# One encoder layer in fp32: attention steps grouped anew, VectorE's order written out at the start of the first FFN, its last four pairs narrow

## The chip, the cores and the metric

The kernel runs on one core of a Trainium2 chip. The metric is the device time of one execution in microseconds (us), the median of several runs. TensorE (PE) does the matmuls into eight PSUM banks, ScalarE (ACT) and VectorE (DVE) work on what lies in SBUF and PSUM, GpSimd (POOL) and SyncE (SP) mostly issue DMAs.

## The reference

One layer on 512 tokens of width 1024: a SwiGLU FFN of hidden width 2816 at half weight, two attention branches side by side, and a second FFN. Each sub-layer has an RMSNorm before and after.

```python
def _swiglu(x, w_gate, w_up, w_down):
    return (jax.nn.silu(x @ w_gate) * (x @ w_up)) @ w_down
...
        f = _swiglu(_rmsnorm(x, ffn1_pre_g[l]), ffn1_w_gate[l], ffn1_w_up[l], ffn1_w_down[l])
        x = x + 0.5 * _rmsnorm(f, ffn1_post_g[l])
        h = _rmsnorm(x, mix_pre_g[l])
        proj = h @ w_in[l]
        qa, ka, va, qb, kb, vb, gate_a, gate_b = jnp.split(proj, splits, axis=-1)
        ha = (B, T, NA_HEADS, HEAD_DIM)
        ya = _neighbourhood_attention(qa.reshape(ha), ka.reshape(ha), va.reshape(ha), na_rpb[l]) @ w_branch_a[l]
        yb = _dilated_mixture(qb, kb, vb, slopes) @ w_branch_b[l]
        merged = jax.nn.sigmoid(gate_a) * ya + jax.nn.sigmoid(gate_b) * yb
        x = x + _rmsnorm(merged @ w_out[l], mix_post_g[l])
        f = _swiglu(_rmsnorm(x, ffn2_pre_g[l]), ffn2_w_gate[l], ffn2_w_up[l], ffn2_w_down[l])
        x = x + 0.5 * _rmsnorm(f, ffn2_post_g[l])
```

The neighbourhood branch has 8 heads of width 64, the dilated one 12 heads in three groups with dilations 1 (the near group), 4 and 16 (the far groups). All values are float32.

## The kernel before, in words

**Arithmetic.** Every fp32 operand is split into a rounded part `hi` and a rest `lo`: ACT casts `hi` (L116) and DVE subtracts it (L117). A product is then three matmuls, hi x hi, hi x lo and lo x hi (`mm3`, L207 to L209).

**FFN, gate and up.** Of the 22 blocks of hidden features (each 128 wide) the first two are computed in the plain way (`proj_first`, `proj_into`). The other 20 go through `seven`: each gate and up projection is treated as a 2 x 2 block product done with seven block products instead of eight, numbered 1 to 7. Their left sides are sums of weight blocks, made partly by DMAs that add onto what they load (POOL, L407 and L408) and partly by DVE in `sums_of` (L413 `t2`, L415 or L418 `t4`). `ready(j, i)` splits block i of pair j; `product(j, i, ...)` runs it. A pair keeps two banks, `q` and `p`. Product 5 starts `p`, ACT copies it (L496) and product 3 adds onto it. Products 6 and 7 and then 4 add onto `q`; DVE reads `q` after product 7 (L490) before product 4 goes on. In the first FFN pairs 0 to 3 have their product 1 done ahead (`first_products`), into four banks.

A *wide* product (5 and 3 alone) has the hi and lo halves of its moving side next to each other: four matmuls of 512 columns (L458) and four of 256 (L460), and DVE then has two more adds a pair (L492, L514). A *narrow* one is twelve matmuls of 256 columns. In the first FFN pairs 0 to 3 are narrow and 4 to 19 wide (`state["narrow"] = 4`), in the second all are wide.

**FFN, down.** `down` does the down projection in the same seven-product way, in class `Blocks`. While the last pairs run, `behind(lead)` and `behind(far)` load and split its first blocks. The rows `ta`, `tb`, `ba`, `bb` are kept in the room of the normalised input `hn`, whose last reader is product 4 of the last pair. For block product 6 DVE adds the rows `ba` onto `ta` (L749); the sums of tokens `v` are L739.

**Attention.** Work of the attention is put in a list, `pend`, as small steps; `step(n)` takes n of them. Between two projections (24 matmuls of 512 columns each) `pair` calls `step`. A step is a burst of scores for two heads (`na_sc`, `g_sc`: 24 matmuls on 64 rows, L1099, four banks, which DVE drains in eight L1106), the transposes of one head's probabilities (`na_tr`, L1133, two banks) or its product with the values (`na_pv`, L1160, one bank). Scores of the far groups (`scores_narrow`, L1071) take two banks a head. An empty step is written as a function that does nothing. `v_far` projects the values of the far groups into four banks, `v_near` those of the near group.

**Order.** A planner lays out each engine's instructions by a simulated timeline, with program order as priority. Stretches in the list `ordered` keep the written order on PE, ACT and DVE; entries of `pool` keep it for the engines that they name; SP keeps it up to the end of the first FFN. `mark()` notes a place in the program.

Of the kernel before, what the change touches and what calls it, by code (L numbers as in the profile page):

```python
# [24 lines left out]
NF = 2816 // P  # L25
# [4 lines left out]
WIDE = (5, 3)  # L30
# [5 lines left out]
STD = 2  # L36
# [10 lines left out]
def block_kernel(ctx, tc, x, gains, weights, rpb_near, rpb_all, alibi0, alibi12, out):  # L47
# [13 lines left out]
    def unit(dt=F32, name="u"):  # L61
        return up.tile([P, 512], dt, tag="u", name=name)
# [61 lines left out]
    ordered = []  # L124
    pool = []
# [65 lines left out]
    def mark():  # L191
        return len(nc.cur_bb.bb.instructions)
# [229 lines left out]
        split(w[:, :512], w[:, 512:], raw)  # L422
        return w

    def seven(use, mv, n_pairs, n0, behind, far, lead, raws, early):

        blocks = {}
        o = {}

        def get(j):
            if j < n_pairs and j > 2:
                raws[j] = load_blocks(n0, j)
            elif j >= n_pairs:
                behind(far)

        def ready(j, i):  # L440
            if j < n_pairs:
                if j and loads:
                    loads.popleft()()
                if i == 1:
                    sums_of(raws[j])
                if j >= EARLY or i not in (1, 2):
                    blocks[j, i] = split_block(raws[j].pop(i))
            else:
                behind(lead)

        def product(j, i, key, start):
            if start:
                o[key, j] = bank(key)
            w = blocks.pop((j, i))
            acc = o[key, j][:, :256]
            if i in WIDE and j >= state["narrow"]:
                for k in range(4):
                    nc.tensor.matmul(o[key, j], w[:, k * P:(k + 1) * P], mv[i][k][2], start=start and k == 0, stop=False,  # L458
                                     skip_group_check=True)
                    nc.tensor.matmul(acc, w[:, 512 + k * P:512 + (k + 1) * P], mv[i][k][0], start=False,  # L460
                                     stop=k == 3, skip_group_check=True)
                return o[key, j]
            for k in range(4):
                mm3(acc, w[:, k * P:(k + 1) * P], w[:, 512 + k * P:512 + (k + 1) * P], *mv[i][k][:2],
                    start and k == 0, k == 3, skip_group_check=True)
            return acc

        res = {}
        get(0)
        get(1)  # L470
        for i in (1, 5, 2, 6, 3, 7, 4):
            ready(0, i)
        for j in range(n_pairs + 1):
            now, was = j < n_pairs, j > 0
            get(j + 2)
            if now:
                if j < EARLY:
                    o["q", j], g = early[j]
                    q = o["q", j][:, :256]
                else:  # L480
                    q = product(j, 1, "q", True)
                    g = unit(name="g")
                    nc.scalar.copy(g[:, :256], q)
                u = unit(name="up")
                res[j] = g, u, u[:, 256:] if j < state["narrow"] else unit(name="p5")
            ready(j + 1, 1)
            if was:
                q0 = product(j - 1, 7, "q", False)
                g0, u0, s0 = res.pop(j - 1)
                nc.vector.tensor_tensor(u0[:, 256:], s0[:, :256], q0, op=ALU.subtract)  # L490
                if j > state["narrow"]:
                    nc.vector.tensor_tensor(u0[:, 256:], u0[:, 256:], s0[:, 256:], op=ALU.add)  # L492
            ready(j + 1, 5)
            if now:
                p = product(j, 5, "p", True)
                nc.scalar.copy(res[j][2], p)  # L496
            ready(j + 1, 2)
            if now and j >= EARLY:
                r = product(j, 2, "r", True)
                nc.vector.tensor_tensor(g[:, :256], g[:, :256], r, op=ALU.add)  # L500
            ready(j + 1, 6)
            if now:
                product(j, 6, "q", False)
                nc.scalar.copy(u[:, :256], q)
            ready(j + 1, 3)
            if was:
                product(j - 1, 4, "q", False)
                use(j - 1, g0, u0, q0)
            ready(j + 1, 7)
            if now:  # L510
                product(j, 3, "p", False)
                nc.vector.tensor_tensor(u[:, :256], p[:, :256], u[:, :256], op=ALU.subtract)  # L512
                if j >= state["narrow"]:
                    nc.vector.tensor_tensor(u[:, :256], p[:, 256:], u[:, :256], op=ALU.add)  # L514
            ready(j + 1, 4)

# [74 lines left out]
    def ffn(g, store, src):  # L591
# [20 lines left out]
        def use(j, pg, pu):  # L612
            h = unit(name="h")
            nc.scalar.activation(h, pg, AF.Silu)
            times(j, pu, h)

        def use7(j, g, u, q):
            if j >= EARLY:
# [14 lines left out]
        for j in range(STD):  # L633
            ps = [bank(), bank()]
            for i in range(2):
                (proj_into if i or j else proj_first)(ps[i], take(False), 0, T)
                next(sums)
                if j < STD - 1:
                    fetch()
            use(j, *ps)  # L640
            if j == 0:
                ordered[-1].append(mark())
        g_post, g_pre = gain(g), None if store else gain(g + 1)
        if not store:
            bias_plan()
# [2 lines left out]

        far, lead, rest = down(m, after, duos, hidden, g_post, g_pre, store, src)
        state["next"] = state["take"] = after + 2 * m + 2  # L650
        state["narrow"] = 0 if store else 4
        seven(use7, mv, NF - STD, n0, lambda q: [f() for f in q.popleft()], far, lead, raws, early)
        rest()

    def parts_of(raw):
# [564 lines left out]
    def mixing(g):  # L1220
# [48 lines left out]
        def na_use(p, pq, pk):  # L1269
            if p < 3:  # L1270
                load_tables(na_tab[p + 1], 3, bias_f[:, (p + 1) * 1536:(p + 2) * 1536])
            parts = qk_parts("na", pq, pk)
            for h in (2 * p, 2 * p + 1):
                pend.append((lambda: None) if h % 2 else lambda h=h: na_sc(parts, h))
                if h > 0:
                    pend.append(lambda h=h: na_tr(h - 1))
                if h > 1:
                    pend.append(lambda h=h: na_pv(h - 2))


        g_tab = {0: [], 1: [], 2: [], 3: []}
# [34 lines left out]
        def g_use(j, pq, pk):  # L1316
            g, p = divmod(j, 2)
            parts = qk_parts(g, pq, pk)
            for h in (2 * p, 2 * p + 1):
                pend.append((lambda: None) if g == 0 and h % 2 else lambda h=h: g_sc(g, parts, h))  # L1320

        def g_tr(g, h):
            pr = hold.pop(("p", g, h))
# [9 lines left out]
        vva += next(v_na)  # L1333
        g_post, g_pre = gain(g), gain(g + 1)
        pair(na_use, 2, 1)
        pair(na_use, 3, 3)
        pend.append(lambda: na_tr(7))
        pend.append(lambda: na_pv(6))
        pend.append(lambda: na_pv(7))
        load_tables(g_tab[0], 3, alibi0[:, :1536])  # L1340
        load_tables(g_tab[1], 3, alibi0[:, 1536:])
        load_tables(g_tab[2], 1, alibi12[:, :512])
        load_tables(g_tab[3], 1, alibi12[:, 512:])
        for j in range(6):
            pair(g_use, j, 1 if j else 3)
        pend.append(lambda: joint(1))
        vvb[1], vvb[2] = v_far()
        vvb[0] = v_near()
# [413 lines left out]
```

## Time and profile before

| | |
|---|---|
| Median of 3 runs | 1078.69 us (1078.28 to 1079.77) |
| Profiled execution, whole | 1078.63 us |
| Its span, first to last instruction | 1076.9 us |
| Mean granted TensorE clock | 0.999 |
| PE busy | 1067.4 us (99%), 6403 matmuls |
| DVE busy | 845.1 us (78%) |
| ACT busy | 650.9 us (60%) |

A row of the timeline gives the start and the duration in us, the engine, the line, the operation and what it writes and reads; in brackets stands the idle time of the engine before it and what ended that. Matmuls overlap, so the time that one costs is read from the start of the next and not from its duration. The pairs of the first FFN lie at 46 to 245 us, its down projection from 233 on, the attention's projections at about 345 to 560, the second FFN from about 742.

### The profile page before, as it was taken

What the parts mean: (1) busy time and instruction counts of PE and PEld (TensorE: products, weight loads), DVE (VectorE), ACT (ScalarE), POOL (GpSimd) and SP (SyncE); (2) the same over time, 40 slices, a digit from 0 to 9 for tenths busy, and PEclk for the clock granted to TensorE, in tenths of its full rate; (3) what the DMA queues carried; (4) which work ended last, traced back from release to release, by engine and by line L of the source; (5) the groups of instructions that cost most, each with busy time, mean ns of one, the idle gap of its engine ahead of it and who ended that gap; (6) DMA issues with size and microseconds to landing.
All of it is one profiled execution on the core that took longest, in us unless ns stands there. A gap on an engine that the chain in (4) does not pass through costs nothing.

```text
span 1076.9 us, 17914 instructions
## 1 busy us (share of the span) xinstructions
PE 1067.4 (99%) x6403; PEld 949.6 (88%) x6403; DVE 845.1 (78%) x1632; ACT 650.9 (60%) x1312; POOL 179.4 (17%) x247
## 2 busy tenths in 40 slices
PE   9999999999999999999999999999999999999997
PEld 7899999997888988888988888889899999998886
DVE  7989888878997667666677654777998888889985
ACT  7646665664784656556676651366655665666672
POOL 4111212014334000000000001133302111104301
PEclk9999999999999999999999999999999999999999
DMA  9979888569994453422232239575938777769962
GB/s 330 198 185 248 218 225 219 148 163 278 231 276 125 125 184 127 135 82 79 80 95 89 79 100 306 139 139 191 292 76 206 190 171 195 192 190 237 221 211 78
DMA packets 95724, 189.80 MB, mean 176 GB/s; under 512 B 24081, under 2 KB 26641, under 8 KB 95634
## 3 DMA queue, kind: packets, MB, share of 16 engines
q1 hardware_dynamic: 68320, 134.18, 36.9%
q0 software_dynamic: 24624, 54.01, 28.1%
q8 instruction: 50, 0.82, 0.3%
q10 hardware_dynamic: 2690, 0.46, 0.2%
q14 instruction: 40, 0.33, 0.1%
HBM read 183.58 MB, written 7.58 MB: 178 GB/s over the span
## 4 chain that ended last, share of the span: by engine, by line
PE 92%; DMA 3%; DVE 2%; SPq 2%; issue 1%; ACT 1%; DVEq 0%; ACTq 0%
PE q L209 11%; PE q L207 11%; PE q L208 11%; PE ps L207 10%; PE ps L208 10%; PE ps L209 10%; PE p L458 6%; PE p L460 3%; PE r L209 3%; PE r L208 3%; PE r L207 3%; PE c L209 2%; PE c L207 2%; PE c L208 2%; SPq L1190 1%; PE ps L1133 1%
## 5 line engine op out<-in xcount | busy, mean ns | idle before, releaser
L117 DVE TENSOR_TENSOR w<-raw,w 128x512 fp32r<-128x512 f32 (+1 forms) x138 | 125.6, 915 | 91.9 <-ACT w L116 88.8
L116 ACT CAST w<-raw 128x512 fp32r<-128x512 f32 (+1 forms) x138 | 110.0, 803 | 93.6 <-PE ps L208 44.1
L207 PE MATMUL ps<-hn,w 128*128 128x512 f32 (+1 forms) x360 | 136.5, 379 | 0.3
L209 PE MATMUL ps<-hn,w 128*128 128x512 f32 (+1 forms) x360 | 134.6, 374 | 0.0
L208 PE MATMUL ps<-hn,w 128*128 128x512 f32 (+1 forms) x360 | 134.3, 373 | 0.0
L116 ACT CAST w<-t 128x512 fp32r<-128x512 f32 x160 | 97.5, 619 | 44.3 <-DVE t L413 28.6
L117 DVE TENSOR_TENSOR w<-t,w 128x512 fp32r<-128x512 f32 x160 | 109.3, 690 | 13.5 <-ACT w L116 11.2
L458 PE MATMUL p<-v,w 128*128 128x512 f32 x288 | 104.5, 397 | 0.0
L208 PE MATMUL q<-v,w 128*128 128x256 f32 x320 | 90.4, 283 | 0.0
L207 PE MATMUL q<-v,w 128*128 128x256 f32 x320 | 90.4, 283 | 0.0
L209 PE MATMUL q<-v,w 128*128 128x256 f32 x320 | 90.0, 283 | 0.0
L407 POOL DMA_DIRECT2D t<-in_weights_dram x40 | 35.0, 874 | 285.5 <-DVE up L512 58.9
L208 PE MATMUL q<-hn,w 128*128 128x256 f32 x288 | 81.6, 283 | 0.0
L209 PE MATMUL q<-hn,w 128*128 128x256 f32 x288 | 81.6, 283 | 0.0
L207 PE MATMUL q<-hn,w 128*128 128x256 f32 x288 | 81.3, 283 | 0.0
L460 PE MATMUL p<-v,w 128*128 128x256 f32 x288 | 80.7, 281 | 0.0
L209 PEld LDWEIGHTS ps<-hn,w 128*128 128x128 f32 x360 | 67.8, 188 | 12.7 <-DVE w L117 0.7
L207 PEld LDWEIGHTS ps<-hn,w 128*128 128x128 f32 x360 | 67.9, 189 | 11.9 <-DVE nast L1106 0.7
L208 PEld LDWEIGHTS ps<-hn,w 128*128 128x128 f32 x360 | 67.9, 189 | 11.0
L458 PEld LDWEIGHTS p<-v,w 128*128 128x128 f32 x288 | 54.2, 188 | 9.6
L207 PEld LDWEIGHTS q<-v,w 128*128 128x128 f32 x320 | 60.9, 191 | 0.3
L208 PEld LDWEIGHTS q<-v,w 128*128 128x128 f32 x320 | 61.0, 191 | 0.1
(328 smaller groups left out, 3015.7 us busy)
## 6 DMA issues: line engine op xcount, KB each, us to landing
raw<-in_weights_dram SPq DMA_DIRECT2D x90, 512.0 KB
t<-in_weights_dram SPq DMA_DIRECT2D x88, 256.0 KB
t<-in_weights_dram POOLq DMA_DIRECT2D x80, 256.0 KB, 5.7
w<-in_weights_dram SPq DMA_DIRECT2D x40, 256.0 KB
rows<-in_weights_dram SPq DMA_DIRECT2D x32, 256.0 KB
w<-in_weights_dram POOLq DMA_DIRECT2D x32, 256.0 KB, 6.3
tb<-in_weights_dram POOLq DMA_DIRECT2D x12, 512.0 KB, 7.7
rows<-in_weights_dram POOLq DMA_DIRECT2D x24, 256.0 KB, 10.9
```

Source lines behind the costliest of these rows:

```text
L116: nc.scalar.copy(hi, src)
L117: nc.vector.tensor_tensor(lo, src, hi.bitcast(F32), op=ALU.subtract)
L207: nc.tensor.matmul(o, sh, mh, start=start, stop=False, **kw)
L208: nc.tensor.matmul(o, sh, ml, start=False, stop=False, **kw)
L209: nc.tensor.matmul(o, sl, mh, start=False, stop=stop, **kw)
L407: nc.gpsimd.dma_start(t1, weights[gate][:, :512], accum_op=ALU.add)
L458: nc.tensor.matmul(o[key, j], w[:, k * P:(k + 1) * P], mv[i][k][2], start=start and k == 0, stop=False, skip_group_check=True)
L460: nc.tensor.matmul(acc, w[:, 512 + k * P:512 + (k + 1) * P], mv[i][k][0], start=False, stop=k == 3, skip_group_check=True)
L1133: nc.tensor.transpose(ps[:, i * P:(i + 1) * P], s, ident)
L1190: nc.sync.dma_start(bias_r[i][:, r, :].rearrange("h (u k) -> h u k", k=8), (rpb_near, rpb_all)[i][:, :, 7 - r:15 - r])
```

## The change

- In `seven` the first pair's block 5 is split ahead of the pair's sums, and `put`, the last multiplication of the plain blocks (`times`, L603), goes between the splits of blocks 3 and 7. Before, it stood ahead of all of them. This holds for both FFNs.
- In the first FFN alone DVE keeps the written order from the first plain block to the second pair's sums (`pin`).
- `state["wide"]` takes the place of `state["narrow"]`: in the first FFN pairs 4 to 15 are wide, 16 to 19 are narrow now; the second stays wide throughout.
- The neighbourhood branch's steps are grouped by a written plan, one group between two projections, and the empty steps of the near group go. By that plan bursts of scores stand in groups of their own.

```diff
--- before.py
+++ after.py
@@ -422,7 +422,7 @@
         split(w[:, :512], w[:, 512:], raw)
         return w
 
-    def seven(use, mv, n_pairs, n0, behind, far, lead, raws, early):
+    def seven(use, mv, n_pairs, n0, behind, far, lead, raws, early, put, pin):
 
 
 
@@ -453,7 +453,7 @@
                 o[key, j] = bank(key)
             w = blocks.pop((j, i))
             acc = o[key, j][:, :256]
-            if i in WIDE and j >= state["narrow"]:
+            if i in WIDE and j in state["wide"]:
                 for k in range(4):
                     nc.tensor.matmul(o[key, j], w[:, k * P:(k + 1) * P], mv[i][k][2], start=start and k == 0, stop=False,
                                      skip_group_check=True)
@@ -468,8 +468,13 @@
         res = {}
         get(0)
         get(1)
-        for i in (1, 5, 2, 6, 3, 7, 4):
+        blocks[0, 5] = split_block(raws[0][5])
+        ready(0, 1)
+        raws[0].pop(5)
+        for i in (6, 3, 7, 4):
             ready(0, i)
+            if i == 3:
+                put()
         for j in range(n_pairs + 1):
             now, was = j < n_pairs, j > 0
             get(j + 2)
@@ -482,13 +487,15 @@
                     g = unit(name="g")
                     nc.scalar.copy(g[:, :256], q)
                 u = unit(name="up")
-                res[j] = g, u, u[:, 256:] if j < state["narrow"] else unit(name="p5")
+                res[j] = g, u, unit(name="p5") if j in state["wide"] else u[:, 256:]
             ready(j + 1, 1)
+            if pin and j == 0:
+                pool.append((pin, mark(), (mybir.EngineType.DVE,)))
             if was:
                 q0 = product(j - 1, 7, "q", False)
                 g0, u0, s0 = res.pop(j - 1)
                 nc.vector.tensor_tensor(u0[:, 256:], s0[:, :256], q0, op=ALU.subtract)
-                if j > state["narrow"]:
+                if j - 1 in state["wide"]:
                     nc.vector.tensor_tensor(u0[:, 256:], u0[:, 256:], s0[:, 256:], op=ALU.add)
             ready(j + 1, 5)
             if now:
@@ -510,7 +517,7 @@
             if now:
                 product(j, 3, "p", False)
                 nc.vector.tensor_tensor(u[:, :256], p[:, :256], u[:, :256], op=ALU.subtract)
-                if j >= state["narrow"]:
+                if j in state["wide"]:
                     nc.vector.tensor_tensor(u[:, :256], p[:, 256:], u[:, :256], op=ALU.add)
             ready(j + 1, 4)
 
@@ -612,7 +619,7 @@
         def use(j, pg, pu):
             h = unit(name="h")
             nc.scalar.activation(h, pg, AF.Silu)
-            times(j, pu, h)
+            return lambda: times(j, pu, h)
 
         def use7(j, g, u, q):
             if j >= EARLY:
@@ -637,9 +644,12 @@
                 next(sums)
                 if j < STD - 1:
                     fetch()
-            use(j, *ps)
+            put = use(j, *ps)
+            if j < STD - 1:
+                put()
             if j == 0:
                 ordered[-1].append(mark())
+        pin = None if store else ordered[-1][1]
         g_post, g_pre = gain(g), None if store else gain(g + 1)
         if not store:
             bias_plan()
@@ -648,8 +658,8 @@
 
         far, lead, rest = down(m, after, duos, hidden, g_post, g_pre, store, src)
         state["next"] = state["take"] = after + 2 * m + 2
-        state["narrow"] = 0 if store else 4
-        seven(use7, mv, NF - STD, n0, lambda q: [f() for f in q.popleft()], far, lead, raws, early)
+        state["wide"] = range(NF - STD) if store else range(4, NF - STD - 4)
+        seven(use7, mv, NF - STD, n0, lambda q: [f() for f in q.popleft()], far, lead, raws, early, put, pin)
         rest()
 
     def parts_of(raw):
@@ -1270,12 +1280,14 @@
             if p < 3:
                 load_tables(na_tab[p + 1], 3, bias_f[:, (p + 1) * 1536:(p + 2) * 1536])
             parts = qk_parts("na", pq, pk)
-            for h in (2 * p, 2 * p + 1):
-                pend.append((lambda: None) if h % 2 else lambda h=h: na_sc(parts, h))
-                if h > 0:
-                    pend.append(lambda h=h: na_tr(h - 1))
-                if h > 1:
-                    pend.append(lambda h=h: na_pv(h - 2))
+            sc = lambda: na_sc(parts, 2 * p)
+            plan = (((sc,), (), ((na_tr, 0),)),
+                    (((na_tr, 1),), (sc,), ((na_pv, 0),), ((na_pv, 1), (na_tr, 2))),
+                    (((na_tr, 3),), (sc,)),
+                    (((na_pv, 2),), ((na_pv, 3), (na_tr, 4)), ((na_tr, 5),), (sc,), ((na_pv, 4),),
+                     ((na_pv, 5), (na_tr, 6)), ((na_tr, 7),), ((na_pv, 6), (na_pv, 7))))
+            for group in plan[p]:
+                pend.append(lambda group=group: [f() if callable(f) else f[0](f[1]) for f in group])
 
 
         g_tab = {0: [], 1: [], 2: [], 3: []}
@@ -1317,7 +1329,8 @@
             g, p = divmod(j, 2)
             parts = qk_parts(g, pq, pk)
             for h in (2 * p, 2 * p + 1):
-                pend.append((lambda: None) if g == 0 and h % 2 else lambda h=h: g_sc(g, parts, h))
+                if g or h % 2 == 0:
+                    pend.append(lambda h=h: g_sc(g, parts, h))
 
         def g_tr(g, h):
             pr = hold.pop(("p", g, h))
@@ -1333,16 +1346,13 @@
         vva += next(v_na)
         g_post, g_pre = gain(g), gain(g + 1)
         pair(na_use, 2, 1)
-        pair(na_use, 3, 3)
-        pend.append(lambda: na_tr(7))
-        pend.append(lambda: na_pv(6))
-        pend.append(lambda: na_pv(7))
+        pair(na_use, 3, 1)
         load_tables(g_tab[0], 3, alibi0[:, :1536])
         load_tables(g_tab[1], 3, alibi0[:, 1536:])
         load_tables(g_tab[2], 1, alibi12[:, :512])
         load_tables(g_tab[3], 1, alibi12[:, 512:])
         for j in range(6):
-            pair(g_use, j, 1 if j else 3)
+            pair(g_use, j, 1)
         pend.append(lambda: joint(1))
         vvb[1], vvb[2] = v_far()
         vvb[0] = v_near()
```

## The prediction

> **What bounds the kernel now.** I read the head of the page first, then TensorE's waits, then the rows around each wait. The page has TensorE (PE) busy for 99% of the span:
>
> ```profile
> PE 1067.4 (99%) x6403; PEld 949.6 (88%) x6403; DVE 845.1 (78%) x1632; ACT 650.9 (60%) x1312; POOL 179.4 (17%) x247
> ...
> PEld ps L207 <- DVE nast L1106: 0.7, 2, 0.4
> ```
>
> The end is set by the sum of the matmuls; VectorE (DVE, 78%) and ScalarE (ACT, 60%) matter only where a matmul finds its operand or its PSUM bank not ready. A gain can come only out of such places. The waits view lists few: past the start two of PE itself (they stand in brackets in the next rows), and some of its weight loads, of which the one quoted is in attention. A matmul's duration hides part of a wait, since it is longer than its step, so I read steps: start to next start in the timeline. Here are all places of this kind that the change can touch, with undisturbed rows between them to measure against:
>
> ```profile
> 49.53 0.28 PE L207 MATMUL q<-v,w 128*128 128x256 f32 x1
> 49.65 0.28 PE L208 MATMUL q<-v,w 128*128 128x256 f32 x1
> 50.48 0.39 PE L207 MATMUL p<-v,w 128*128 128x256 f32 x1 [0.56 <-ACT w L116]
> 50.70 0.28 PE L208 MATMUL p<-v,w 128*128 128x256 f32 x1
> ...
> 231.91 0.40 PE L458 MATMUL p<-v,w 128*128 128x512 f32 x1
> ...
> 233.32 0.40 PE L207 MATMUL r<-w,a 128*128 128x512 f32 x1
> ...
> 265.41 0.39 PE L207 MATMUL c<-w,pair 128*128 128x512 f32 x1
> 265.64 0.39 PE L208 MATMUL c<-w,pair 128*128 128x512 f32 x1
> 267.16 0.50 PE L209 MATMUL c<-w,pair 128*128 128x512 f32 x1 [1.13 <-DVE pair L117]
> 267.50 0.39 PE L207 MATMUL c<-w,pair 128*128 128x512 f32 x1
> ...
> 422.66 1.09 PE L1133 MATMUL ps<-ident,u 128*128 128x128 f32 x8
> 423.90 0.50 PE L207 MATMUL ps<-hn,w 128*128 128x512 f32 x1
> 424.24 0.39 PE L208 MATMUL ps<-hn,w 128*128 128x512 f32 x1
> ...
> 458.11 1.04 PE L1133 MATMUL ps<-ident,u 128*128 128x128 f32 x8
> 458.90 0.47 PE L207 MATMUL ps<-hn,w 128*128 128x512 f32 x1
> ```
>
> Undisturbed: a 256-column step is 0.12 us (49.53 to 49.65) though its duration reads 0.28, and a 512-column step 0.23 (265.41 to 265.64). A narrow product, twelve matmuls of 256 columns, is 12 x 0.12 = 1.44 us. A wide one, four of 512 and four of 256, runs from 231.91 to 233.32: 1.41 us.
>
> Place A, first pairs of the first FFN: 49.65 to 50.48 is 0.83 instead of 0.12, and the next step 0.22: 0.71 + 0.10 = 0.81 us lost. Place B, start of its down projection: 265.64 to 267.16 is 1.52 instead of 0.23, the next 0.34: 1.29 + 0.11 = 1.40 us. Place C: eight transposes right behind a burst of scores take 1.24 us until the projection goes on (422.66 to 423.90), and 0.79 where no burst stands before them (458.11 to 458.90): 0.45 us. The quoted wait has two such places, 0.7 us by the loads' count, so C is 0.7 to 2 x 0.45 = 0.9; I take 0.8. A + B + C = 3.0 us is nearly all that there is to gain.
>
> **The change part by part.** *Narrow products in pairs 16 to 19 of the first FFN* (N). Products 5 and 3 of four pairs, eight products: 8 x (1.44 - 1.41) = +0.24 us on PE, which is never idle there, so it lands whole. Taken off DVE are two 256-column adds a pair (L492, L514), off ACT half of one copy (L496), and one unit buffer a pair. DVE is off the path in these pairs, so the relief itself is worth nothing; it counts by what it brings forward at B.
>
> The rule that speaks against this part is in the Trainium skill, "TensorE: Matmul & The Clock Gate", section Back-to-back issue gap: it gives a sustained spacing of about 81 ns at 128 columns and 131 ns at 512. Drawn straight between, 256 columns would be 98 ns (my estimate), a narrow product 1.17 us against 0.92 wide, and the eight would cost +2.1 us. The trace does not agree: its 512-column step is 0.23.
>
> *What place B hangs on.* DVE's rows at the end of the pairs and after, with the same stretch of the second FFN last; then PE's and SyncE's:
>
> ```profile
> 239.54 0.42 DVE L490 TENSOR_TENSOR up<-p,q 128x256 f32<-128x256 f32 x1
> ...
> 252.02 1.22 DVE L749 TENSOR_TENSOR ta<-ta,ba 128x1024 f32<-128x1024 f32 x1 [2.39 <-DMA ba<-in_weights_dram]
> 254.65 1.23 DVE L749 TENSOR_TENSOR ta<-ta,ba 128x1024 f32<-128x1024 f32 x1 [1.40 <-DMA ba<-in_weights_dram]
> ...
> 968.75 1.29 DVE L739 TENSOR_TENSOR v<-h 128x512 f32<-128x512 f32 x2
> ...
> 981.93 1.23 DVE L749 TENSOR_TENSOR ta<-ta,ba 128x1024 f32<-128x1024 f32 x1 [1.46 <-DMA ba<-in_weights_dram]
> ```
>
> ```profile
> 244.53 0.28 PE L209 MATMUL q<-hn,w 128*128 128x256 f32 x1
> ...
> 244.73 0.88 SPq L710 DMA_DIRECT2D ba<-in_weights_dram  x2
> ```
>
> Before product 4 of the last pair may add onto its bank, L490 must have read product 7's sum there, and L490 stands in DVE's queue until 239.54, behind adds and splits. So TensorE's order has down-projection work first and product 4 last, to 244.53. That product is the last reader of `hn`, whose room `ba` takes: SyncE issues `ba` at 244.73, DVE gets it at 252.02, and having both L749 ahead of the splits in its queue it stands idle for 2.39 + 1.40 us before them. What it then still has to split comes too late for PE at 267.16. In the second FFN, with the same work, v (968.75) is ahead of L749, and PE has no wait. By the queue as it stands, dropping one L514 (0.33 us) brings L490 forward by so much, and PE's order hides that: B = 0. With the queue set anew, as it is wherever the instructions on it change, 1.40 us of splits need only slip into 3.8 us of idle time: B = -1.40. The second FFN's rows are the nearest, so I take -1.40 and keep 0 for the range.
>
> *DVE's written order to the second pair's sums* (A). DVE's rows, then ACT's, ahead of place A:
>
> ```profile
> 44.40 1.29 DVE L413 TENSOR_TENSOR t<-t,w 128x512 f32<-128x512 f32 x2
> 45.61 1.29 DVE L415 TENSOR_TENSOR t<-t,t 128x512 f32<-128x512 f32 x2
> ...
> 48.78 1.65 ACT L116 CAST w<-t 128x512 fp32r<-128x512 f32 x3
> ```
>
> DVE makes both pairs' sums (two L413, two L415) before it splits block 6 of the first pair, and ACT has casts of later blocks at 48.78, whose end (50.43) PE awaits. In the written order one L413 and one L415 stand ahead of block 6, so the first pair's splits come half of 1.29 + 1.29, 1.3 us, earlier, and the second pair's sums behind block 4. What waits behind the pinned instructions is the second pair's blocks 6 and 4, used two products (2 x 1.44 us) later or more: hidden. `put` (L603) moves between the splits of 3 and 7; it frees a bank that nobody stands for. No DMA passes another on SyncE's queue; GpSimd's accumulating loads for later pairs, which wait on those sums, slip by some splits and are used pairs later. I take A = -0.81; ends 0 and -0.81, and +0.5 if the pin makes a split stand behind an ACT cast.
>
> *Attention's groups* (C). The neighbourhood bursts of heads 2, 4 and 6 come one, two and four projections later, and those of 4 and 6 now stand alone between two projections, not ahead of transposes, so the next projection finds a bank. Gone: 0.8 us. Their transposes and products follow under projections; the last product of the branch comes one projection later than now. Each split-off place gets an edge more; the nearest row is the step from 423.90 to 424.24, 0.34 instead of 0.23, so 2 x 0.11 = +0.2. C = -0.6; ends -0.9 and, if the bank waits only move, +0.2. The first near-group burst moves one projection later, so that one lies between it and the second and not two; the narrow score steps and the store of their statistics, on ACT's queue, come one step earlier, under projections that PE has anyway.
>
> *Second FFN's start.* The same reordering without the pin; no PE wait there now, so 0, and I set +0.3 for new small stalls in all queues that are set anew (the two steps around 50.48 show what one costs, 0.1 to 0.7).
>
> Sum: 0.24 - 1.40 - 0.81 - 0.6 + 0.3 = -2.3. The profiled execution took 1078.63 us, 0.06 under the median 1078.69. 1078.63 - 2.3 = **1076.3 us**.
>
> **The rivals.**
> *B stays* (`ba` late, splits still behind L749): for it speaks that DVE's relief near the place is one add of 0.33 us; against it the second FFN. Then -2.3 + 1.4 = -0.9: 1077.7.
>
> *A or C only moves*: a bank or a cast is late one product further on. That costs 0.6 to 0.8 of the gain: 1077.0.
>
> *Slower: the two near-group bursts, now one projection apart, run PSUM out.* The projection of the far values opens four banks right behind the second burst, with two free: 6 matmuls x 0.23 = 1.4 us of cover. DVE drains a burst in eight L1106, of which this is one, and then has the last pair's q and k splits:
>
> ```profile
> 505.21 0.42 DVE L1106 CUSTOM_DVE_ANT_0 u<-ps,table 128x256 f32<-128x256 f32 x1
> ```
>
> A drain is at most 8 x 0.42 = 3.4 us. If another drain's length of work stands ahead of the second's, PE waits up to 3.4 + 3.4 - 1.4 = 5.4 us: 1081.7. It decides from 2.3 us of waiting. Against it: one projection, 24 x 0.23 = 5.5 us, lies between the bursts, more than a drain.
>
> *Slower: weight loads bare.* A narrow product loads weights twelve times, a wide one eight. By the page's head a load is at least 949.6 / 6403 = 0.148 us; uncovered, a narrow product is 12 x 0.148 = 1.78 against 1.41, and eight cost +3.0 in place of +0.24: 1079.1. The 0.12 steps of narrow products say no. The skill's spacing above belongs beside it; by it the time would be 1078.2.
>
> **How the numbers follow.** All three places as summed: 0.42, time 1076.3 (own range 1075.5 to 1077.1). B stays 0.28, A or C only moves 0.20, PSUM out 0.07, bare loads or the skill's spacing 0.03. About 0.2% (2.16 us) is what a measurement of this kernel can tell from no change, so faster means under 1076.5: most of the first case (0.33) and a little of the third (0.03), 0.36. Slower means over 1080.9: part of the PSUM case, and what I have not thought of, 0.08. Within: 0.56. The range 1075.3 to 1078.7 leaves out the slow cases and 0.1 of tails.
>
> **What would show it.** Right: the waits view without `c L209 <- DVE pair` and `p L207 <- ACT w`; product 4 of the last pair soon behind product 7, `ba` issued before 244; L749 after v in DVE's queue; every group of eight transposes about 0.8 us; near-group bursts one projection apart without a wait at the far values. Wrong: new PE waits on DVE L1106 near 505, on `w` in the second FFN's first pairs, or on `pair` again.

## The result, and the profile after

The changed kernel takes 1077.14 us (median of 22 runs, 1076.85 to 1077.75), the kernel before in runs beside it 1078.59 us (22 runs, 1077.6 to 1081.92). The ratio is 0.9986, 95% interval [0.998, 0.9993]: a gain of 1.45 us. The interval lies below 1, but the gain is inside the 0.2% (2.16 us) that the prediction takes for what a measurement can tell from no change. Predicted were 1076.3 us, with a range of 1075.3 to 1078.7.

The profiled execution took 1077.08 us with a span of 1075.3 us (1076.9 before); the granted clock is 0.998 (0.999). First the head of its page, then one of TensorE's waits (total, times, longest):

```profile
PE 1067.7 (99%) x6435; PEld 952.3 (89%) x6435; DVE 843.1 (78%) x1624; ACT 649.3 (60%) x1312; POOL 178.6 (17%) x247
...
PE ps L207 <- DVE u L1188: 0.4, 1, 0.4
```

6435 matmuls are the 6403 of before and four more for each of eight narrow products; eight adds are gone from DVE. Of the waits of before, that for `pair` and that for `w` are gone. A wait for `u` at a projection of attention is new. Code lines up to L470 stand where they stood; those up to L639 are 7 higher (L512 is L519), those behind mostly 10 (L739 is L749, L1099 is L1109).

Where the time went is read from the start of the same instruction in both traces, from the first matmul of the first FFN to the last instruction:

| Stretch | Before, us | After, us | Difference |
|---|---|---|---|
| up to the first matmul of the first FFN | 10.43 | 9.85 | -0.57 |
| on to the first wide product | 60.07 | 59.27 | -0.80 (A) |
| wide pairs, on to the first `r` | 162.82 | 163.12 | +0.30 (N) |
| on to the rows behind the down projection | 102.44 | 100.86 | -1.57 (B) |
| on to the third attention pair | 57.77 | 57.78 | +0.01 |
| attention, on to the gates | 149.40 | 150.57 | +1.17 (C) |
| gates, second FFN, end | 533.93 | 533.84 | -0.08 |

The first row is not the change: over all the profiles here this stretch took 9.73 to 11.36 us, whatever the kernel. Without it the trace shows -0.98 us. Three of the table's borders as TensorE's rows, first of after, then those of before that have not been shown:

```profile
69.12 0.40 PE L458 MATMUL p<-v,w 128*128 128x512 f32 x1
...
232.25 0.40 PE L207 MATMUL r<-w,a 128*128 128x512 f32 x1
...
390.89 0.48 PE L207 MATMUL ps<-hn,w 128*128 128x512 f32 x1
...
541.46 0.40 PE L207 MATMUL ps<-hn,w 128*128 128x512 f32 x1
```

```profile
70.50 0.40 PE L458 MATMUL p<-v,w 128*128 128x512 f32 x1
...
393.53 0.48 PE L207 MATMUL ps<-hn,w 128*128 128x512 f32 x1
...
542.92 0.40 PE L207 MATMUL ps<-hn,w 128*128 128x512 f32 x1
```

232.25 - 69.12 = 163.13 against 233.32 - 70.50 = 162.82; 541.46 - 390.89 = 150.57 against 542.92 - 393.53 = 149.39.

**Attention after.** TensorE's rows around the two near-group bursts (L1109, 24 matmuls on 64 rows), the products of heads 6 and 7 with the values (L1170) ahead of and inside the first, and the first narrow score steps (L1081):

```profile
484.75 1.60 PE L1170 MATMUL ps<-u 128*128 128x256 f32 x12
...
490.74 0.28 PE L1170 MATMUL ps<-u 128*128 128x256 f32 x1
...
491.88 0.38 PE L1109 MATMUL ps<-k,q 64*128 64x256 f32 x1
492.19 0.62 PE L1170 MATMUL ps<-u 128*128 128x256 f32 x3
492.74 1.69 PE L1109 MATMUL ps<-k,q 64*128 64x256 f32 x23
494.82 0.50 PE L207 MATMUL ps<-hn,w 128*128 128x512 f32 x1 [0.39 <-DVE u L1188]
...
500.49 2.03 PE L1109 MATMUL ps<-k,q 64*128 64x256 f32 x24
502.45 0.62 PE L207 MATMUL ps<-w,hn 128*128 128x512 f32 x1
...
509.73 0.40 PE L1081 MATMUL ps<-k,q 128*128 128x256 f32 x2
509.96 0.51 PE L207 MATMUL ps<-w,hn 128*128 128x512 f32 x1
510.31 0.40 PE L1081 MATMUL ps<-k,q 128*128 128x256 f32 x2
```

Head 7's product of eight matmuls is torn into 4 (in the x12), 1 and 3, and the burst into 1 and 23. The projection behind it then finds no bank: it waits until DVE has read head 7's product. The second burst runs from 500.49 to 502.45, 1.96 us. The narrow score steps stand in twos, and the projection's step between these two is 0.35 us (509.96 to 510.31) where undisturbed ones are 0.23 to 0.24. The same two bursts before, one row of each with the row behind it:

```profile
490.13 1.69 PE L1099 MATMUL ps<-k,q 64*128 64x256 f32 x24
491.75 0.50 PE L207 MATMUL ps<-hn,w 128*128 128x512 f32 x1
...
502.85 1.69 PE L1099 MATMUL ps<-k,q 64*128 64x256 f32 x24
504.47 0.63 PE L207 MATMUL ps<-w,hn 128*128 128x512 f32 x1
```

Both are whole and take 1.62 us. So this is where part of the gain went; the experiments ask whether it is the tearing or the bursts' nearness, and whether the other parts stand by themselves.

### The profile page after: what moved, and what is told of

It reads as the page before. It is cut to its first block, busy times and chain, and to the rows that moved or that the text cites. A ratio compares the mean times of both kernels' runs of the same rounds, so it can differ in the third digit from the quotient of the medians.

```text
span 1075.3 us, 17988 instructions
## 1 busy us (share of the span) xinstructions
PE 1067.7 (99%) x6435; PEld 952.3 (89%) x6435; DVE 843.1 (78%) x1624; ACT 649.3 (60%) x1312; POOL 178.6 (17%) x247
## 4 chain that ended last, share of the span: by engine, by line
PE 99%; DVE 0%; ACT 0%; issue 0%; DVEq 0%; ACTq 0%
PE q L209 11%; PE q L207 11%; PE q L208 11%; PE ps L207 11%; PE ps L209 11%; PE ps L208 10%; PE p L458 6%; PE p L460 3%; PE r L208 3%; PE r L209 3%; PE r L207 3%; PE c L207 2%; PE c L209 2%; PE c L208 2%; PE q L273 1%; PE ps L1143 1%
## 5 line engine op out<-in xcount | busy, mean ns | idle before, releaser
L458 PE MATMUL p<-v,w 128*128 128x512 f32 x256 | 93.1, 397 | 0.0
L460 PE MATMUL p<-v,w 128*128 128x256 f32 x256 | 71.7, 281 | 0.0
L207 PE MATMUL q<-w,a 128*128 128x512 f32 x156 | 60.9, 390 | 0.0
```

Of the source, the lines that this page charges most:

```text
L207: nc.tensor.matmul(o, sh, mh, start=start, stop=False, **kw)
```

## The experiments

The theory: the parts add up; the parts of the FFN gain about 2.0 us and the new attention groups lose about 1.2. Rivals: the parts hang on each other (queues set anew by one feed the other), or the loss is in the lone bursts as such. Differences "in the trace" are those of the table above, against the profiled execution before. They leave out the stretch up to the first FFN.

**One part at a time.** First all of the change but its attention groups:

```diff
 # the changed kernel, with the kernel before's na_use, g_use and pair(..., 3)
-            plan = (((sc,), (), ((na_tr, 0),)),
...
+                pend.append((lambda: None) if h % 2 else lambda h=h: na_sc(parts, h))
```

> Both FFN parts of the change, attention grouped as before. Theory 1 (the FFN parts gain, the new attention groups lose 1.2 us): from the traces of before and after, 0.8 us gained at the first pairs, 1.5 at the down projection, 0.3 lost by narrow products: 2.0 us under the kernel before, some 1076.6, and so faster than the whole change by about 1.2. Theory 2 (the whole change's parts hang together, the planner sets attention's order by what the FFN leaves it): attention's order and cost change too, no clear 1.2 us between this and the whole change.

Measured: 1076.24 us, ratio 0.9981 [0.9972, 0.999]; in the trace -0.80 at A, +0.30 at N, -1.58 at B, 0.00 in attention: -2.07 in all. Next the kernel before with the attention groups alone (the same edit the other way round):

> Only attention grouped anew, the FFNs as before. Theory 1: the two waits behind scores and transposes (0.86 us) are gone, but the near group's bursts cost more: 1.2 us over the kernel before, some 1079.9. Theory 2: attention by itself gains the forecast 0.6 us, 1078.0, and the loss in the whole change came from the FFN's shift.

Measured: 1079.21 us, ratio 1.0009 [1.0001, 1.0018]; attention +1.18, as in the changed kernel. The profiled execution took 1080.27 us, the slowest of the 11, and in it two stretches that the edit doesn't touch moved too: the down projection with its wait for `pair` is 0.32 us longer, and 0.50 us went ahead of the third attention pair, on a wait that comes back below. TensorE's waits:

```profile
PE c L209 <- DVE pair L117: 1.1, 1, 1.1
PE p L207 <- ACT w L116: 0.6, 1, 0.6
PE ps L207 <- DVE u L1178: 0.4, 1, 0.4
PE ps L1133 <- DVE u L1121: 0.3, 1, 0.3
```

The first two are B and A, still there; the third is the new one in attention, the fourth the one ahead of the third pair. Then the two parts of the FFN apart, narrow products alone and the written order alone:

```diff
 # narrow_only: the kernel before and
-        state["narrow"] = 0 if store else 4
+        state["wide"] = range(NF - STD) if store else range(4, NF - STD - 4)
```

> Only the last four pairs of the first FFN narrow. Theory 1 (relief of VectorE lets product 4 of the last pair run sooner, ba is issued sooner and the splits are in time): eight products cost 0.3, the wait of 1.4 to 1.5 us at the start of the down projection is gone: 1.2 us under the kernel before, some 1077.4. Theory 2 (that wait went because the order at the start shifted everything behind it): 0.3 us over before, and the wait for pair stands.

```diff
 # order_only: the first run of this section and
-        state["wide"] = range(NF - STD) if store else range(4, NF - STD - 4)
+        state["wide"] = range(0 if store else 4, NF - STD)
```

> Only the order at the start: block 5 split first, put behind block 3's split (both FFNs), VectorE's written order in the first FFN. Theory 1: the 0.8 us at 50.48 are gone and nothing else: some 1077.8, the wait for pair at the down projection stands (1.4 us). Theory 2: the shift reaches the down projection, and that wait goes too: some 1076.4.

Measured: narrow alone 1077.09 us, ratio 0.9988 [0.998, 0.9997], +0.27 at N, -1.58 at B, -0.01 at A (and +0.12 ahead of the third attention pair). Order alone 1077.58 us, ratio 0.9992 [0.9983, 1.0], -0.78 at A, +0.03 at N, and the wait for `pair` stays, with the down projection 0.53 us shorter in this profile. So A belongs to the order, N and B to the narrow products, C to the groups, and the parts add up: the FFN parts' -2.07, and from the run with the groups alone +1.18 in attention and -0.07 behind it, make -0.96, against -0.98 in the changed kernel.

**What in attention costs.** Untorn: the transposes of heads 6 and 7 each a step earlier and their products a step apart, bursts still one projection apart.

```diff
-                     (((na_pv, 2),), ((na_pv, 3), (na_tr, 4)), ((na_tr, 5),), (sc,), ((na_pv, 4),),
-                     ((na_pv, 5), (na_tr, 6)), ((na_tr, 7),), ((na_pv, 6), (na_pv, 7))))
+                     (((na_pv, 2),), ((na_pv, 3), (na_tr, 4)), ((na_tr, 5),), (sc,), ((na_pv, 4), (na_tr, 6)),
+                     ((na_pv, 5), (na_tr, 7)), ((na_pv, 6),), ((na_pv, 7),)))
```

> The changed kernel with one thing undone: the transposes of heads 6 and 7 each go one step earlier and the products of heads 6 and 7 a step apart, so that nothing of head 7 is due in the projection between the two near-group bursts that can be split by them. The near-group bursts stay one projection apart. Theory (head 7's products, due right behind its transposes, tore the first near-group burst): the burst is whole again, the wait of a projection on the DVE's read of head 7's product is gone: 0.85 to 1.3 us under the changed kernel, ratio to the kernel before 0.9974 to 0.9979. Rival (PSUM runs short because the bursts stand one projection apart): the changed kernel's time within 0.3 us, the loss shows at or behind the second burst.

Measured: 1075.59 us, ratio 0.9978 [0.9969, 0.9987]; attention 148.92 us, 1.65 under the changed kernel. TensorE's rows:

```profile
492.33 1.69 PE L1109 MATMUL ps<-k,q 64*128 64x256 f32 x24
493.95 0.50 PE L207 MATMUL ps<-hn,w 128*128 128x512 f32 x1
...
499.61 1.69 PE L1109 MATMUL ps<-k,q 64*128 64x256 f32 x24
501.23 0.63 PE L207 MATMUL ps<-w,hn 128*128 128x512 f32 x1
```

Both bursts are whole and take 1.62 us again, one projection apart. No projection waits for the bank of head 7's product, and nearness by itself costs nothing: from the third attention pair up to the far values this run takes 110.25 us and the run below, with the bursts two projections apart, 110.23. Of the gain, 1.31 us lie up to the far values, with the second burst's 0.34 us among them. The other 0.34 us lie behind, because the narrow score steps are torn less here. That makes the gain larger than was expected. The edit moves two things, the transposes and products of heads 6 and 7 in time and the two products apart; which of them keeps the burst whole was not run by itself.

Far values: one empty step behind the second burst, so that the narrow score steps come one step later.

```diff
                 if g or h % 2 == 0:
                     pend.append(lambda h=h: g_sc(g, parts, h))
+            if j == 1:
+                pend.append(lambda: None)
```

> The changed kernel with one empty step behind the second near-group burst, so that the narrow score steps of the far groups come one step later, as in the kernel before, and stand whole in groups of four. Nothing else differs. Theory (each torn step pays about 0.12 us at each of its extra edges between tiles): 0.4 to 0.6 us under the changed kernel, in the projection of the far values alone; ratio to the kernel before 0.9980 to 0.9983. Rival (edges between tiles cost nothing, the time there is a wait for a bank): no difference over 0.15 us there.

Measured: 1076.52 us, ratio 0.9988 [0.998, 0.9997]; attention 0.55 us under the changed kernel, all of it from the far values on. The interval doesn't tell it from the changed kernel, the trace does. Its narrow steps are mostly whole; the first of them:

```profile
513.86 0.64 PE L1081 MATMUL ps<-k,q 128*128 128x256 f32 x4
```

Both remedies, and the bursts two projections apart:

```diff
-                    (((na_pv, 2),), ((na_pv, 3), (na_tr, 4)), ((na_tr, 5),), (sc,), ((na_pv, 4),),
-                     ((na_pv, 5), (na_tr, 6)), ((na_tr, 7),), ((na_pv, 6), (na_pv, 7))))
+                    (((na_pv, 2),), ((na_pv, 3), (na_tr, 4)), (sc,), ((na_tr, 5),), ((na_pv, 4), (na_tr, 6)),
+                     ((na_pv, 5), (na_tr, 7)), ((na_pv, 6),), None, ((na_pv, 7),)))
...
+                if group is None:
+                    pend.append(lambda: near.popleft()())
+                    continue
...
```

(`near` holds the first near-group burst.)

> The changed kernel's first FFN as it is; in attention the lone bursts of scores stay, but the first near-group burst comes one projection earlier (two projections between the near-group bursts, with the products of head 7 under the projection between), head 6's scores come ahead of head 5's transposes, and an empty step stands behind the second near-group burst, so that every burst and every set of eight transposes is whole. Theory (attention's 1.2 us are lost at the torn near-group burst, at the second one behind it and at the torn narrow score steps): attention 0.5 to 0.9 us shorter than in the kernel before instead of 1.2 longer, so 1.7 to 2.1 us under the changed kernel: a ratio to the kernel before of 0.9968 to 0.9972. Rival (bursts of scores alone between two projections cost by themselves, wherever they stand): attention stays 0.5 to 1.2 us longer than before, ratio 0.998 to 0.9987.

Measured: 1075.44 us (1075.17 to 1075.74), ratio 0.9978 [0.9969, 0.9987]; attention 148.70 us, 0.70 under the kernel before and 1.87 under the changed one. No wait of TensorE's matmuls is left in attention. So lone bursts gain, by about what the prediction summed for them, once the bursts are whole.

**What A hangs on.** The written order, but VectorE not held to it:

```diff
-            if pin and j == 0:
+            if False:
```

> The kernel before with the written order of the first FFN's start as in the changed kernel (block 5 first, put between the splits of 3 and 7), but without holding VectorE to it; all products wide, attention as before. Theory (the 0.81 us come from holding DVE's order; without that its queue has both pairs' sums ahead of block 6's split again): the wait p on w by ACT's cast near 50 us is back, 0.0 us gained in the first pairs, ratio 0.9997 to 1.0003. Rival (the written order alone sets ACT's casts early enough): minus 0.8 us there, ratio 0.9990 to 0.9994.

Measured: 1077.87 us, ratio 1.0001 [0.9992, 1.001]; -0.01 at A. TensorE's waits show both stalls of before again, 0.9 us for `pair` and that of A:

```profile
PE p L207 <- ACT w L116: 0.6, 1, 0.6
```

Without the hold the written order does nothing. Whether a hold of the order of before would do as well was not run. The down projection is 0.35 us shorter here than before though nothing in it was changed; its wait for `pair` reads 0.7 to 1.1 us over the runs that keep it.

**What B hangs on.** One narrow pair and not four:

```diff
 # the run with the narrow products alone and
-        state["wide"] = range(NF - STD) if store else range(4, NF - STD - 4)
+        state["wide"] = range(NF - STD) if store else range(4, max(4, NF - STD - 1))
```

> The kernel before with narrow products 5 and 3 in the last pair alone (two products and not eight). Theory (what removes the wait for pair is that the last pair's product 4 comes earlier in TensorE's order, so that ba is issued about 3 us earlier; that hangs on the last pair's sums alone): the wait is gone as with four narrow pairs, minus 1.54 us in the down projection, and the narrow products cost a quarter, plus 0.06 to 0.08 us in place of 0.27 to 0.30: minus 1.45 us, ratio 0.9985 to 0.9988. Rival (DVE needs the relief of all four pairs to be early enough): the wait for pair stays, wholly or in part, minus 0 to 0.7 us.

Measured: 1076.68 us, ratio 0.9987 [0.9978, 0.9995]; -1.58 at B, +0.07 at N. A quarter of the price buys all of it. Then no narrow product at all, but DVE's written order in the down projection held, first over fourteen of the 34 block products of its loop:

```diff
             for n, s in enumerate(seq):
...
+                if not store and n == 0:
+                    pinned = mark()
+                if not store and n == 14:
+                    pool.append((pinned, mark(), (mybir.EngineType.DVE,)))
```

> The kernel before, all products wide as in it, with only DVE's order in the first FFN's down projection held as it is written, so that the splits of v and pair come ahead of both additions onto ta that need ba. TensorE's order and the place of ba's load are as in the kernel before (ba issued at about 244.7). Theory (the queue's order, splits behind the additions that stand for ba, makes TensorE wait for pair): the wait at about 267 is gone without a narrow product, minus 1.1 to 1.5 us against the kernel before, ratio 0.9986 to 0.9990. Rival (what counts is that ba is issued 3 us earlier, which only the narrow products bring): the wait stays or moves to the next operand that hangs on ta, ratio 0.9997 to 1.0003.

Measured: 1082.30 us, ratio 1.0039 [1.0027, 1.0052], slower. The wait for `pair` is gone as the theory had it, but in the trace the down projection is 3.92 us longer, which neither side expected. TensorE's waits:

```profile
PE q L207 <- ACT part L801: 1.9, 1, 1.9
...
PE q L209 <- DVE a L117: 0.8, 2, 0.5
```

Held so far, DVE does its splits one block after the other and stands for ACT's cast ahead of many of them: for `a` alone 4.9 us in eight places of the down projection, against 1.4 us in one place before. Later operands come late. So the hold was cut to the second to eighth product (`n == 1` and `n == 7` in the diff above):

> The kernel before, all wide, with DVE's written order held over a short stretch only, from the second to the eighth product of the first FFN's down projection, where it has pair's first split and one split of ta ahead of the two additions onto ta, and not over the whole stretch as in the run that cost 5 us at later operands. ba is issued as in the kernel before. Theory (it is the order in DVE's queue, not the time of ba): the wait for pair at about 267 is gone, minus 1.2 to 1.5 us there, and behind it less is lost than under the long hold: between minus 1.5 and plus 1.0 us in the down projection. Rival (only an earlier ba removes it): a wait for pair or for a split of ta of 0.5 us or more within 5 us of that place.

Measured: 1077.17 us, ratio 0.9995 [0.9986, 1.0004]. The interval holds 1, so the time by itself doesn't show the gain. The trace does: -1.45 at B, and no wait of TensorE's matmuls in its place. DVE's rows, then SyncE's:

```profile
246.62 0.69 DVE L117 TENSOR_TENSOR pair<-v,pair 128x512 fp32r<-128x512 f32 x1 [0.69 <-ACT pair L116]
...
251.97 1.23 DVE L749 TENSOR_TENSOR ta<-ta,ba 128x1024 f32<-128x1024 f32 x1 [2.32 <-DMA ba<-in_weights_dram]
...
256.06 1.22 DVE L749 TENSOR_TENSOR ta<-ta,ba 128x1024 f32<-128x1024 f32 x1
...
262.65 0.69 DVE L117 TENSOR_TENSOR pair<-v,pair 128x512 fp32r<-128x512 f32 x1
```

```profile
244.36 1.10 SPq L710 DMA_DIRECT2D ba<-in_weights_dram  x2
```

`ba` is issued at 244.36 (244.73 before, with the FFN starting 0.35 us later; 241.80 after) and DVE still stands for it, 2.32 us. But splits lie between and ahead of the two additions, the last split of `pair` ends at 263.3, and TensorE needs it at about 267. So the order of the queue alone removes B, with `ba` no earlier. The narrow products bring `ba` forward as well.

**Together.** The hold at the first FFN's start, the short hold in the down projection with all products wide, and the attention of the run with both remedies:

> The parts that the runs point to, together: DVE's written order held at the first FFN's start (minus 0.81 us), DVE's order held over the second to the eighth product of its down projection with all products wide (minus 1.45, nothing for narrow products), and attention with whole near-group bursts two projections apart (minus 0.69). Theory (the places are independent, so their parts add up): minus 2.9 to 3.0 us against the kernel before from the first product of the first FFN to the end, about 1.4 us under the changed kernel, ratio to the kernel before 0.9970 to 0.9975 with its interval. Rival (queues set anew at one place give back elsewhere): less than 2.5 us of gain from the first product on, with a new wait of TensorE named in the waits.

Measured: 1075.84 us (11 runs, 1074.94 to 1076.60), ratio 0.9979 [0.997, 0.9988]. In the profiled execution the gain is 1.64 us, not 2.9: -0.77 at A, -1.24 at B, -0.70 in attention, and +1.01 ahead of the third attention pair. There TensorE waits in the transposes; the rows are TensorE's and ACT's:

```profile
391.43 0.98 PE L1147 MATMUL ps<-ident,u 128*128 128x128 f32 x7 [0.46 <-DVE u L1135]
```

```profile
375.58 1.05 ACT L116 CAST w<-raw 128x1024 fp32r<-128x1024 f32 x1 [1.15 <-DMA raw<-in_weights_dram]
```

ACT stands for weights out of DRAM, for 1.15 us here; in the kernel before the idle time at that place is 0.34 us and TensorE has no such wait. Two other profiles have the same: the run with the groups alone (ACT 1.11 us, TensorE +0.50 us) and that with the long hold (1.08 and +0.51). In the other eleven ACT stands 0.5 us or less there and TensorE doesn't wait. These three kernels have three different attention groupings, and each of the groupings also stands in a profile without the wait, so the groups don't bring it; why the load was late is open. The profiled execution, 1076.60 us, is the slowest of the 11, the fastest took 1074.94, and no other was profiled, so how many have the wait is open too. The expectation that the parts add up fell in this profile; the ratio's interval still holds what was expected, 0.9970 to 0.9975. Against the kernel before, the combination and the run with both remedies can't be told apart.

## Why the prediction was right or wrong, point by point

**N**, predicted +0.24: +0.30 for eight products, +0.27 with the narrow products alone, +0.07 for two, so 0.03 to 0.04 us each, all of it on the path. The sustained spacing of the Trainium skill ("TensorE: Matmul & The Clock Gate", section Back-to-back issue gap), by which the prediction worked out +2.1 us, does not fit this trace, where a 512-column step is 0.23 us. Bare weight loads, at +3.0, fell with the same numbers.

**A**, predicted -0.81: -0.80. The mechanism is the predicted one. DVE's rows and then ACT's of after:

```profile
43.83 0.69 DVE L413 TENSOR_TENSOR t<-t,w 128x512 f32<-128x512 f32 x1
44.55 0.69 DVE L415 TENSOR_TENSOR t<-t,t 128x512 f32<-128x512 f32 x1
45.21 0.69 DVE L117 TENSOR_TENSOR w<-t,w 128x512 fp32r<-128x512 f32 x1
...
48.22 0.69 DVE L413 TENSOR_TENSOR t<-t,w 128x512 f32<-128x512 f32 x1
```

```profile
45.60 1.66 ACT L116 CAST w<-t 128x512 fp32r<-128x512 f32 x3
```

One L413 and one L415 stand ahead of block 6's split at 45.21 (46.81 before; 0.57 us of that are the earlier start of the FFN in this trace), and the second pair's sum comes behind it. From the cast that waits for the first L413, ACT's queue has five casts ahead of its first copy out of `p`, and the last of them ends at 47.26. Before, there were ten, and the last, which TensorE stood for, ended at 50.43.

**B**, predicted -1.40: -1.57, of which 1.40 is the stall that the prediction read. Predicted and seen: product 4 of the last pair comes earlier (from 240.30 on, 243.22 before), `ba` is issued before 244, and no wait for `pair` is left. The sign "L749 after v" tells nothing: DVE's sums of `v` stand ahead of the first L749 (now L759) in the kernel before as well, at 248.34, so the prediction's contrast with the second FFN was misread. What moved is the splits of `pair`. DVE's and SyncE's rows of after, then DVE's splits of `pair` before:

```profile
244.52 1.29 DVE L749 TENSOR_TENSOR v<-h 128x512 f32<-128x512 f32 x2
249.25 1.22 DVE L759 TENSOR_TENSOR ta<-ta,ba 128x1024 f32<-128x1024 f32 x1 [3.44 <-DMA ba<-in_weights_dram]
...
251.53 0.68 DVE L117 TENSOR_TENSOR pair<-v,pair 128x512 fp32r<-128x512 f32 x1
...
253.34 1.22 DVE L759 TENSOR_TENSOR ta<-ta,ba 128x1024 f32<-128x1024 f32 x1
...
262.16 1.29 DVE L117 TENSOR_TENSOR pair<-v,pair 128x512 fp32r<-128x512 f32 x2
```

```profile
241.80 0.87 SPq L720 DMA_DIRECT2D ba<-in_weights_dram  x2
```

```profile
255.79 0.69 DVE L117 TENSOR_TENSOR pair<-v,pair 128x512 fp32r<-128x512 f32 x1
...
266.42 1.29 DVE L117 TENSOR_TENSOR pair<-v,pair 128x512 fp32r<-128x512 f32 x2
```

The first split of `pair` now slips between the two additions, as the prediction had it, and the second addition no longer stands for `ba` (1.40 us before). The first still stands for 3.44 us, but it starts at 249.25 and not at 252.02: `ba` is there earlier as well, which the prediction names among its signs but not in the working of its sum. How much each brings in the changed kernel was not run apart; the short hold shows that the order is enough. Not foreseen: that one narrow pair does what four do. The rival "B stays" fell.

**C**, predicted -0.6: +1.17. This is the step that failed. The term that was worked out, bank waits behind bursts against edges, held: in the run with both remedies attention is 0.70 us shorter than before. What failed is the last sentence of that part, which set two moves at nothing: the near-group bursts one projection apart, and the narrow score steps one step earlier "under projections that PE has anyway". The narrow steps cost 0.55 us: inside the projection of the far values' 512-column matmuls they stand in 8 pieces and not in 3, and the step behind such a piece is 0.11 us longer, five times 0.11. (In the untorn run there are 5 pieces, and 0.21 us.) The pieces further on, among 256-column matmuls, cost nothing. The rest, 1.17 + 0.70 - 0.55 = 1.3 us, lies around the near-group bursts. Of the distance of the bursts the untorn run shows that it is harmless by itself. What the step did not look at was what else falls due there: head 7's transposes and, a step behind them, the products of heads 6 and 7, whose bank the next projection needed. DVE's rows of after show what held that bank, and when the first burst is read:

```profile
492.83 1.23 DVE L117 TENSOR_TENSOR w<-raw,w 128x1024 fp32r<-128x1024 f32 x1 [4.61 <-ACT w L116]
494.09 0.68 DVE L1188 TENSOR_TENSOR u<-ps,u 64x512 f32<-64x512 f32 x1
...
499.19 0.42 DVE L1116 CUSTOM_DVE_ANT_0 u<-ps,table 128x256 f32<-128x256 f32 x1
```

The product's last matmuls start at 492.19; its read starts only at 494.09, behind a weight split. The first burst is read from 499.19 on, 4.8 us after it ended (1.1 us in the untorn run), and this reading is still under way when the second burst starts at 500.49. In the untorn run the second burst's two heads start together; here the second starts three steps behind the first, at 500.83, and these are the 0.34 us. That it stands for a bank which this reading frees is inferred from the times; no wait in the profile names it.

**Allowance for new stalls**, +0.3: the FFN's queues show none, and the second FFN is unchanged within 0.1 us. The rival "A or C only moves" is nearest to what happened, but in C the bank waits went and others came at another place, for another reason. "PSUM out", 5.4 us at the far values, came true in small at most and one step earlier: 0.34 us in the second burst, none at the far values.

The sum by measured parts is 0.30 - 0.80 - 1.57 + 1.17 - 0.07 (the other rows) = -0.97 against -2.3 forecast. The result stands 0.8 us above the forecast, inside the range. C alone was missed by 1.8 us; the unused allowance (0.3), B (0.2) and 0.57 us in the stretch up to the first FFN, which the change doesn't touch, made good the rest. So that the time came so near is in part luck.

## What to carry to other kernels

When steps between matmul streams are regrouped, look at each moved step for its neighbours as well as for the bank that it waits for: here a product due one step behind its transposes came with a torn burst, a bank that was held longer and a drain that came late for the next burst. Price a stall by its steps in the timeline and ask for the cheapest edit that reorders the queue in front of it; here two narrow products, or a hold over a short stretch of the queue, did what eight narrow products did. A hold on an engine's order should cover only the stretch that it is for: the same hold over fourteen block products turned -1.45 us into +3.92.

## What the runs showed of the hardware beyond that

- The stretch up to the first FFN took 9.73 to 11.36 us over 14 profiles: more than any part of this change brought.
- In the kernels that keep the wait for `pair`, the down projection differs by -0.53 to +0.32 us from the profile before. A single profile shows the place of a wait, but its size only roughly.
- A load of weights at attention's start for which ACT stood 0.7 to 0.8 us longer went with 0.5 to 1.0 us lost on TensorE, in three kernels with three different attention groupings, and in none of the other eleven.
